# Expert weights in long rows, items of 32 slots in both layers, and 32-by-32 turns on VectorE

## The chip, the cores and the metric

The kernel runs on one core of a Trainium2 chip. The metric is the device time of one execution in microseconds (us); three timed runs of the kernel before have the median 2958.98 us. The core has TensorE (PE, with its weight loads as PEld), VectorE (DVE), ScalarE (ACT), GpSimd (POOL) and SyncE (SP), whose main work here is to issue transfers, and 16 DMA engines that carry all transfers.

## The reference, cut to what matters

The program is one block of a recurrent and sparse-attention model on 512 tokens of 1024 channels, and then two layers of a second block. Each of these two layers ends in a mixture of 32 experts, and the change lies there alone. In the first of the two layers 768 tokens (512 of the sequence, 256 of the context) go to two experts each, in the second 512 tokens:

```
for each token: the best of 4 groups, in it the 2 best of 8 experts, with two gates
run(xb, e) = (silu(xb @ w1[e]) * (xb @ w3[e])) @ w2[e]
y[token] += gate * run(token, e)
w1, w3: [2, 32, 1024, 512]    w2: [2, 32, 512, 1024]    all float32
```

One expert's weights are 6.29 MB. With the inputs of the reference, counting the routing gives 1536 chosen (token, expert) pairs over all 32 experts in the first layer, between 2 and 154 to an expert, and 1024 pairs over 26 experts in the second, where three experts have 212, 382 and 209.

## The kernel before

`route` (L1563) orders the experts by how many blocks of slots they need, and writes for every item (one block of slots, of one expert) the rows to gather, the rows to scatter to, its expert (`eid`) and whether its weights have to be loaded (`new`). A block has 64 slots in the first layer and 32 in the second (`BLOCK`). The numbers of items in the straight-line code are 41 and 51 (`NSTATIC`), which is just what the routing needs; the loop behind them runs zero times.

`experts` (L1788) works through the items. Even items take experts with many blocks from the front of the list and share one place for weights. Odd items take experts from the end and have two places by turns. A load for odd item i + 4 or even item i + 2 (`ld`) can be issued once item i has used the same piece of that place. Pieces 0 and 1 are halves of w1 and w3, pieces 2 and 3 halves of w2. Every load of a piece is issued by SP in order; where `new` is 0 the transfer is skipped. With the routing above, the first layer has 29 loads in its items, the second 23; three experts more are loaded ahead of each layer's items.

For item i the order on TensorE is: first product (pieces 0, 1; `first`, L1827), then the second product of item i - 1 (pieces 2, 3; `second`, L1843). A gather on POOL brings the item's token rows to `xg`, in ng = 128 / slots parts, so that all 128 partitions are filled. The stationary operands are slices of 64 or 32 columns, and ng such products stand side by side in the columns of the array. Both products need the tokens or the activations with channels on the partition. `turn` (L1816) does this: 128-by-128 transposes on TensorE into PSUM (`tps`), and a copy to SBUF on ACT (`xT`, `aT`). `silu` (L1835) takes one ACT and two DVE operations. `scatter` (L1853) multiplies the result by gate and modulation into `ys` on DVE (L1859), and POOL scatters it (L1860). In the first layer a DVE operation (L1858) writes the modulation into the same `ys` buffer beforehand; there are ng + 1 such buffers.

The order of instructions on each engine is that of a scheduler, except where `pin` keeps the program's order.

Of the kernel before, what the change touches and what calls it, by code (L numbers as in the profile page):

```python
# [11 lines left out]
F32 = mybir.dt.float32  # L12
# [12 lines left out]
BLOCK = (64, 32)  # L25
NSTATIC = (41, 51)
NIMAX = 64
# [5 lines left out]
def constants():  # L33
# [20 lines left out]
    # for the routing: 0.., order of experts, 8.., 256 (token tile - 128), offsets of the parts of rows, 2 p, p;  # L54
    # the work block of an item: a + total * b - places of the second lane * c
# [14 lines left out]
class Stream:  # L70
    """Column chunks of weights [1024, 256 each], split into (hi, lo) by halves of their rows, a half
    ahead of the products; the last ones are only loaded. The chunks asked for count from a base."""
# [33 lines left out]
class Kern:  # L106
# [16 lines left out]
    def rsqrt(self, pool, v, scale, eps):  # L123
        """1/sqrt(v*scale+eps) for a [128, 1] tile: a bit guess and three Newton steps, each on a
        multiple c of the root (c becomes -2 c^3), divided out in the end."""
# [21 lines left out]
    def mm3(self, out, stat, mov, start, stop):  # L147
        """out += stat.T @ mov with each side a (hi, lo) pair."""
        nc = self.nc
        (sh, sl), (mh, ml) = stat, mov  # L150
        nc.tensor.matmul(out, sh, mh, start=start, stop=False)  # L151
        nc.tensor.matmul(out, sh, ml, start=False, stop=False)  # L152
        nc.tensor.matmul(out, sl, mh, start=False, stop=stop)  # L153
# [13 lines left out]
    def wchunk(self, ap, kt, cols, pool=None, raw=None):  # L167
        """A [kt*128, cols] piece of a weight as a list of kt (hi, lo) pairs [128, cols]."""
# [68 lines left out]
    def vectors(self, z, engine):  # L237
        """Per-channel vectors with the channel on the partition."""
# [15 lines left out]
    def norm_hT(self, pool, x, gain, hi, lo, work):  # L254
        """rmsnorm of x [128, 4, 1024] (token, channel), transposed to (hi, lo) [128, 8, 512]."""
# [39 lines left out]
    def proj(self, w, N=512):  # L295
        """The two 128-channel tiles of a 256-column chunk as [channel, token] in PSUM."""
# [10 lines left out]
    def projg(self, W, c, N):  # L307
        """The same from a stream, in steps."""
# [12 lines left out]
    def fill(self):  # L321
        """One step of work that is not tied to the place where it runs."""
        if self.bg is not None:
            next(self.bg, None)
# [11 lines left out]
    def mixer(self):  # L336
        nc, tc, a = self.nc, self.tc, self.a
        with ExitStack() as st:
# [21 lines left out]
            # gates: 0.5 * sigmoid, [token, tile, 48]  # L360
# [45 lines left out]
    def keys(self, m):  # L406
        """Keys of groups 2m, 2m+1 with (hi, hi) and (lo, lo) stacked."""
# [16 lines left out]
    def compress(self, kp):  # L424
        """Compressed keys (hi, hi / lo, lo stacked) and values (two copies of the 32 rows)."""
# [57 lines left out]
    def gelu2(self, out, x, pool, shape, tag):  # L483
        """2 * gelu(x) (tanh form); x in SBUF."""
# [7 lines left out]
    def pair(self, t, Q, KD):  # L492
        """Heads 2t and 2t+1: half the gated sum of the three branches, [channel, token]."""
# [4 lines left out]
        # compressed branch  # L498
# [34 lines left out]
        # the two dense branches  # L533
# [43 lines left out]
    def rnn_vectors(self):  # L577
# [11 lines left out]
        # softplus(-lam) = max(-lam, 0) + log1p(exp(-|lam|)), exp as ((1+t)/(1-t))^16 with t = tanh(-|lam|/32)  # L589
# [9 lines left out]
        # log1p(e) = 2 atanh(z), z = e / (2 + e) <= 1/3  # L599
# [21 lines left out]
    def rnn(self, c, yA):  # L621
        """Channels 256c..: conv, RG-LRU and the mixing gates; the sum with yA to y (hi, lo)."""
# [22 lines left out]
        for m in range(2):  # L645
# [9 lines left out]
            # y = (1 + exp(log_a)) / 2 is about 1/(1-th), th = tanh(log_a / 2), and one Newton step makes it so  # L655
# [5 lines left out]
            # a = (1+th)/(1-th), sqrt(1-a^2) = 2 sqrt(-th)/(1-th)  # L661
# [23 lines left out]
    def row(self, pool, name, ap, n=D, engine=None):  # L685
        """A vector on all partitions."""
# [4 lines left out]
    def mix_out(self, xb):  # L691
        """x + rmsnorm(y @ w_out)."""
# [17 lines left out]
    def norm_add(self, x, o, g, pool):  # L710
        """x += rmsnorm(o) * g for one token tile."""
# [66 lines left out]
    def ple(self):  # L778
        """x + sigmoid(x @ w_gate + b) * (p @ w_proj), by [channel, token]; leaves x and its transpose."""
# [48 lines left out]
    def modulation(self, pool, pp, pt_pool):  # L828
        """silu(c) @ w_ada + b_ada for both conditionings, a step at a time: by rows in DRAM
        (modd) and by channel on the partition (modT)."""  # L830
# [58 lines left out]
    def mcol(self, l, r, n):  # L889
        """Modulation vector n of layer l and conditioning r, channel on the partition: [128, 8]."""  # L890
        return self.modT[l][:, r, 8 * n:8 * n + 8]

    def mrow(self, pool, l, r, n, tag, engine=None):
        """The same on all partitions: [128, 1024]."""
# [11 lines left out]
    def transposeN(self, src, n, j, tag="pp"):  # L906
        """Channel tile j of n token tiles, transposed into PSUM: [128, n * 128]."""
# [5 lines left out]
    def affine_split(self, hi, lo, src, sc, sh, pool):  # L913
        """(hi, lo) of src * sc + sh with per-partition scalars."""
# [81 lines left out]
    def open_route(self, l, NT, pool, kv):  # L996
        """What the routing keeps of each token tile, and the routers' biases."""
# [14 lines left out]
    def logit_parts(self, l, r, wg, c12):  # L1012
        """For the logits of (t scale + shift) gs + bs, which are scale (t @ wg) + shift c1 + c2."""
# [24 lines left out]
    def open_side(self, l, r):  # L1038
        """Tokens of the sequence (r = 0) or of the context (r = 1)."""
# [15 lines left out]
    def side_input(self, c):  # L1055
        """The modulated input, transposed, as (hi, lo); in the second layer with stops after the norms."""
# [40 lines left out]
    def stream(self, l):  # L1097
        """The chunks of w_in_2 and w_out_2 in the order of their use."""
# [3 lines left out]
    def tokpairs(self, W, c, NT):  # L1102
        """[token, 256] products, two token tiles to a PSUM bank."""
# [8 lines left out]
    def rope(self, out, src, i, nh, wk):  # L1112
        """Axial rotary embedding of token tile i: src [128, nh * 64] in PSUM."""
# [656 lines left out]
    def expert_load(self, l, s, n, e, cond=None, engine=None, pin=None):  # L1770
# [8 lines left out]
        for dst, src in prs:  # L1779
            src = src.rearrange("o (k p) c -> p (o k) c", p=128)  # L1780
            if cond is None:
                d = (engine or nc.sync).dma_start(dst, src)
                if pin:
                    pin(d)
# [216 lines left out]
```

## Time and profile before

| | before |
|---|---|
| median of 3 timed runs (lowest to highest) | 2958.98 us (2957.39 to 2959.16) |
| span of the profiled execution | 2959.7 us |
| PE busy, share of the span | 2529.7 us, 85% |
| DVE busy | 1376.6 us, 47% |
| ACT busy | 864.8 us, 29% |
| POOL busy | 446.9 us, 15% |
| bytes moved by DMA | 595.76 MB |
| of these, on SP's queue | 553.08 MB |

The span is the time from the first to the last instruction of one profiled execution; it is 0.7 us above the median of the timed runs. The shares are means over many stages. The two stretches with experts lie at about 1600 to 2106 us and 2470 to 2911 us of the span, and only rows from inside them tell what bounds them. "DMA share" is the mean busy share of the 16 DMA engines. It can pass 1 where packets of two queues overlap. A wait is put down to the event that came last.

### The profile page before, as it was taken

The page shows a single profiled execution, that of the slowest core. Times are in us where ns is not written, and L with a number is a line of the kernel's source. Part 1 is how long each engine was busy: PE and PEld are TensorE (multiplying, and loading weights), DVE is VectorE, ACT ScalarE, POOL GpSimd, SP SyncE. Part 2 cuts the span into 40 slices and gives each one's busy share as a digit, 9 for nine tenths or more (in the row PEclk, how much of TensorE's full clock was granted, in tenths as well). Part 3 has the DMA queues.
Part 4 walks back from the last instruction along what each step waited for, and adds up shares of the span by engine and source line. Part 5 has one row for each costly group of instructions (what it writes and reads, how often), then busy time and mean ns, then how long its engine had stood idle before and what let it go on. Part 6 is the DMA issues. An engine that isn't in the chain of part 4 may idle for free. (4 is left out here: it accounts for less than half of the span.)

```text
span 2959.7 us, 45451 instructions
## 1 busy us (share of the span) xinstructions
PE 2529.7 (85%) x17077; PEld 1696.9 (57%) x17077; DVE 1376.6 (47%) x3629; ACT 864.8 (29%) x1765; POOL 446.9 (15%) x370
## 2 busy tenths in 40 slices
PE   7899999989999979878996999998468986667773
PEld 5767767777776867777783333332157773334441
DVE  4387787653332254777765212111468763111114
ACT  2265665532221123544421111100145421011111
POOL 0010010000100000030022321111130025322212
PEclk9899999999998989889997999999779997988997
DMA  3311212337776222341157999999611167999994
GB/s 119 101 43 61 63 34 72 108 115 227 233 238 213 93 86 77 101 153 44 43 215 279 377 392 410 410 407 408 253 45 58 36 255 277 362 393 370 355 355 172
DMA packets 348716, 595.76 MB, mean 201 GB/s; under 512 B 26948, under 2 KB 180104, under 8 KB 347216
## 3 DMA queue, kind: packets, MB, share of 16 engines
q1 hardware_dynamic: 319040, 553.08, 51.7%
q0 software_dynamic: 14400, 25.59, 2.4%
q10 hardware_dynamic: 15056, 14.17, 1.6%
q8 instruction: 137, 2.24, 0.3%
q14 instruction: 83, 0.68, 0.1%
HBM read 832.37 MB, written 25.92 MB: 290 GB/s over the span
## 5 line engine op out<-in xcount | busy, mean ns | idle before, releaser
L1832 PE MATMUL ph<-r,xT 128*32 128x256 f32 (+1 forms) x4576 | 513.0, 459 | 53.8 <-DMA r<-w 50.9
L157 DVE TENSOR_TENSOR wl<-wr,wh 128x1024 fp32r<-128x1024 f32 (+1 forms) x193 | 236.6, 1230 | 315.5 <-ACT wh L156 313.1
L1832 PEld LDWEIGHTS ph<-r,xT 128*32 128x32 f32 (+1 forms) x4576 | 201.8, 122 | 305.4 <-issue 233.4
L156 ACT ACTIVATE wh<-wr 128x1024 fp32r<-128x1024 f32 (+1 forms) x193 | 202.8, 1055 | 430.4 <-PE pj L152 213.9
L1847 PE MATMUL py<-r,aT 128*32 128x256 f32 (+1 forms) x2288 | 266.5, 475 | 67.7 <-DMA r<-w 67.7
L1847 PEld LDWEIGHTS py<-r,aT 128*32 128x32 f32 (+1 forms) x2288 | 99.6, 124 | 189.4 <-issue 145.3
L1821 ACT ACTIVATE aT<-tps 128x128 f32<-128x128 f32 (+1 forms) x92 | 29.8, 324 | 585.2 <-PE tps L1819 585.2
L1839 DVE SCALAR_TENSOR_TENSOR et<-et,ph 128x128 f32<-128x128 f32 (+1 forms) x92 | 31.8, 346 | 288.8 <-ACT et L1838 288.6
L1813 POOL DMA_INDIRECT xg<-hxd,tok x92 | 96.2, 1046 | 412.0 <-PE tps L1819 380.5
L151 PE MATMUL pj<-hh,wh 128*128 128x512 f32 x384 | 155.6, 406 | 1.7 <-ACT wh L156 1.7
L152 PE MATMUL pj<-hl,wh 128*128 128x512 f32 x384 | 154.0, 401 | 0.0
L153 PE MATMUL pj<-hh,wl 128*128 128x512 f32 x384 | 153.1, 400 | 0.0
L151 PE MATMUL tk<-wh,lh 128*128 128x256 f32 x416 | 130.4, 313 | 19.4 <-DVE k2l L1168 8.0
L1860 POOL DMA_INDIRECT yd<-ys,dst x92 | 93.2, 1013 | 344.0 <-DVE ys L1859 324.6
L1858 DVE SCALAR_TENSOR_TENSOR ys<-g2s,isc,g2s 128x512 f32<-128x512 f32 x41 | 30.6, 751 | 244.3 <-DMA yd<-ys,dst 244.3
L151 PE MATMUL pj<-h2h,wh 128*128 128x512 f32 x352 | 143.5, 408 | 0.1
L153 PE MATMUL pj<-h2h,wl 128*128 128x512 f32 x352 | 139.4, 396 | 0.0
L152 PE MATMUL pj<-h2l,wh 128*128 128x512 f32 x352 | 139.2, 396 | 0.0
L153 PE MATMUL tk<-wh,ll 128*128 128x256 f32 x416 | 127.0, 305 | 2.1 <-DVE ll L157 2.1
L152 PE MATMUL tk<-wl,lh 128*128 128x256 f32 x416 | 127.3, 306 | 0.0
L540 POOL TENSOR_SCALAR B<-dm 128x512 f32<-128x512 f32 x32 | 52.7, 1647 | 451.3 <-DVE z L555 258.2
L1405 POOL TENSOR_SCALAR s2r<-s2r 128x1024 f32<-128x1024 f32 x3 | 8.3, 2775 | 666.9 <-DMA s2r<-modd 666.9
(525 smaller groups left out, 5494.8 us busy)
## 6 DMA issues: line engine op xcount, KB each, us to landing
r<-w SPq DMA_DIRECT2D x580, 1024.0 KB
wr<-w_in SPq DMA_DIRECT2D x48, 1024.0 KB
adw<-w_ada SPq DMA_DIRECT2D x96, 512.0 KB
wr<-ffn_w_gate_up SPq DMA_DIRECT2D x22, 1024.0 KB
wr<-w_out SPq DMA_DIRECT2D x16, 1024.0 KB
wr<-ffn_w_down SPq DMA_DIRECT2D x10, 1024.0 KB
fy<-yd SPq DMA_DIRECT2D x10, 1024.0 KB
wr<-ple_w_gate SPq DMA_DIRECT2D x4, 1024.0 KB
```

The lines of the kernel that those rows point to most:

```text
L151: nc.tensor.matmul(out, sh, mh, start=start, stop=False)
L152: nc.tensor.matmul(out, sh, ml, start=False, stop=False)
L153: nc.tensor.matmul(out, sl, mh, start=False, stop=stop)
L156: self.nc.scalar.activation(hi, src, AF.Copy)
L157: self.nc.vector.tensor_tensor(lo, src, hi.bitcast(F32), op=OP.subtract)
L540: nc.gpsimd.tensor_scalar(B, dm, SLOPE[h], None, op0=OP.mult)
L1813: pin(nc.gpsimd.indirect_dma_start(xg[i % XG], None, hx, bass.IndirectOffsetOnAxis(tokc.bitcast(U32), 0), bounds_check=NT * 128 * ng - 1, ...
L1832: pin(nc.tensor.matmul(H[group(g)], X[:, k % nx, group(k // nx)], R13[s][n][:, q, :, cs], start=k == 0, stop=k == 7, skip_group_check=True))
L1839: nc.vector.scalar_tensor_tensor(t, t, 1.0, H[:, 0:m], op0=OP.add, op1=OP.mult)
L1847: pin(nc.tensor.matmul(Y[group(g)], A[:, k % na, group(k // na)], R2[s][n][:, q, g * CX:(g + 1) * CX], start=k == 0, stop=k == 3, skip_gro ...
L1858: nc.vector.scalar_tensor_tensor(g, g2[1], isc, g2[0], op0=OP.mult, op1=OP.add)
L1860: d = nc.gpsimd.indirect_dma_start(yd, bass.IndirectOffsetOnAxis(dstc.bitcast(U32), 0), ys, None, bounds_check=NT * 256 * ng - 1, oob_is_e ...
```

## The change

Four things are changed together. The weights of the experts are laid out anew on the host (`expert_layout`): w1 and w3 of one half become one array of 128 rows of 4096 numbers (16 KB, where a row in memory was 2 KB before), and half of w2 becomes 128 rows of 2048 numbers (8 KB, 4 KB before), so that a piece is one transfer in place of two for pieces 0 and 1. The rows are ordered for 32-by-32 squares. The first layer gets blocks of 32 slots, as the second has, and 65 items in place of 41; by the routing this makes 30 loads in the items in place of 29. `turn` becomes one DVE instruction that turns each 32-by-32 square in place of transposes on TensorE and a copy on ACT. And the activations are turned right behind `silu`, where before their transposes stood in TensorE's queue behind the first half of the next item's first product.

```
-BLOCK = (64, 32)
-NSTATIC = (41, 51)
-NIMAX = 64
+BLOCK = (32, 32)
+NSTATIC = (65, 51)
+NIMAX = 80
...
         if n < 2:
-            r = slice(n * 512, (n + 1) * 512)
-            prs = [(self.R13[s][n][:, :, z, :], pick(w, r)) for z, w in enumerate(("w1_2", "w3_2"))]
+            dst, src = self.R13[s][n].rearrange("p q z c -> p (q z c)"), a["w13_2"][l][e, n]
         else:
-            prs = [(self.R2[s][n - 2], pick("w2_2", slice((n - 2) * 256, (n - 1) * 256)))]
-        for dst, src in prs:
-            src = src.rearrange("o (k p) c -> p (o k) c", p=128)
+            dst, src = self.R2[s][n - 2].rearrange("p q c -> p (q c)"), a["w2_2"][l][e, n - 2]
+        src = src.rearrange("o p f -> p (o f)")
...
-            def turn(src, n, tag):
-                ps = px.tile([128, 4, 128], F32, name=self.nm("tps"), tag="px")[:, 0:n]
-                for q in range(n):
-                    pin(nc.tensor.transpose(ps[:, q, :], src[:, q * 128:(q + 1) * 128], self.ident))
-                t = ek.tile([128, n, 128], F32, name=self.nm(tag), tag=tag)
-                nc.scalar.activation(t, ps, AF.Copy)
+            def turn(src, tag):
+                w = src.shape[-1]
+                t = ek.tile([128, w // BS, BS], F32, name=self.nm(tag), tag=tag)
+                nc.vector.transpose(t.rearrange("p k s -> p (k s)"), src)
                 return t
...
-                if n == 0 and i > 0:
-                    A[i - 1] = turn(H[i - 1], na, "aT")
                 if n == 1:
-                    H[i] = silu(H[i])
                     if i + 1 < NS:
-                        X[i + 1] = turn(xg[(i + 1) % XG], nx, "xT")
-                    else:
-                        A[i] = turn(H[i], na, "aT")
+                        X[i + 1] = turn(xg[(i + 1) % XG], "xT")
+                    A[i] = turn(silu(H.pop(i)), "aT")
...
+def expert_layout(w1, w3, w2):
+    w13 = np.stack([w1, w3], 3).reshape(2, 32, 4, 2, 4, 32, 2, 512).transpose(0, 1, 3, 2, 5, 4, 6, 7)
+    w2 = np.asarray(w2).reshape(2, 32, 4, 2, 2, 32, 1024).transpose(0, 1, 3, 2, 5, 4, 6)
+    return np.ascontiguousarray(w13).reshape(2, 32, 2, 128, 4096), np.ascontiguousarray(w2).reshape(2, 32, 2, 128, 2048)
```

The order of DVE's instructions in the middle of the first layer's items, before (`ph` is the first product, `et` the activation, `py` the second product; what an instruction waits for stands in brackets, DMASW being a scatter or gather):

```order
L1859 SCALAR_TENSOR_TENSOR ys_15040<-py_15029,gatem,ys_15040 128x512 [waits PE_49]
L1858 SCALAR_TENSOR_TENSOR ys_15265<-g2s_12830,isc,g2s_12829 128x512 [waits DMASW5_49,DVE_49]
L1839 SCALAR_TENSOR_TENSOR et_15093<-et_15093,ph_15049 128x256 [waits Activation_49]
L1840 SCALAR_TENSOR_TENSOR et_15093<-et_15093,ph_15049 128x256 [waits DVE_49]
L1859 SCALAR_TENSOR_TENSOR ys_15115<-py_15104,gatem,ys_15115 128x512 [waits PE_49]
```

And DVE's order at the same place of the changed kernel:

```order
L1856 SCALAR_TENSOR_TENSOR ys_15162<-py_15143,gatem,ys_15162 128x256 [waits PE_49]
L1855 SCALAR_TENSOR_TENSOR ys_15607<-g2s_12830,isc,g2s_12829 128x256 [waits DMASW0_49,DVE_49]
L1818 STREAM_TRANSPOSE xT_15313<-xg_13618 128x256 [waits DMASW1_49,PE_49]
L1836 SCALAR_TENSOR_TENSOR et_15226<-et_15226,ph_15171 128x128 [waits Activation_49]
L1837 SCALAR_TENSOR_TENSOR et_15226<-et_15226,ph_15171 128x128 [waits DVE_49]
L1818 STREAM_TRANSPOSE aT_15230<-et_15226 128x128 [waits DVE_49]
L1856 SCALAR_TENSOR_TENSOR ys_15251<-py_15232,gatem,ys_15251 128x256 [waits PE_49]
```

In both, the operation that prepares a `ys` buffer (L1858, now L1855) stands right behind the one that writes a result (L1859, now L1856). It takes over the buffer of that very result (every third of them before, every fifth now), and so waits for that result's scatter. New is that both turns stand behind it in DVE's queue; `xT` is that of the next item but one after `et`'s.

SP's issues for two neighbouring items of the second layer, before (DMAHW0 to 7 are the eight semaphores that count landings; `r` with 4x512 is half the rows of w1 or of w3, with 2x1024 half of w2; register instructions between the issues are left out):

```order
L1786 DMA r_19534<-w_2 128x4x512 [waits DMAHW5_49,PE_49]
L1786 DMA r_19534<-w_2 128x4x512 [waits DMAHW6_49]
L1786 DMA r_19535<-w_2 128x4x512 [waits DMAHW7_49,PE_49]
L1786 DMA r_19535<-w_2 128x4x512 [waits DMAHW0_49]
L1786 DMA r_20324<-w_2 128x2x1024 [waits DMAHW1_49,PE_49]
L1786 DMA r_20325<-w_2 128x2x1024 [waits DMAHW2_49,PE_49]
...
L1786 DMA r_3259_19848<-w_2 128x4x512 [waits DMAHW3_49,PE_49]
L1786 DMA r_3259_19848<-w_2 128x4x512 [waits DMAHW4_49]
L1786 DMA r_3260_19849<-w_2 128x4x512 [waits DMAHW5_49,PE_49]
L1786 DMA r_3260_19849<-w_2 128x4x512 [waits DMAHW6_49]
L1786 DMA r_19584<-w_2 128x2x1024 [waits DMAHW7_49,PE_49]
L1786 DMA r_19585<-w_2 128x2x1024 [waits DMAHW0_49,PE_49]
```

And for two neighbouring items of that layer in the changed kernel:

```order
L1783 DMA r_22260<-w_2 128x4096 [waits DMAHW3_49,PE_49]
L1783 DMA r_22261<-w_2 128x4096 [waits DMAHW4_49,PE_49]
L1783 DMA r_23045<-w_2 128x2048 [waits DMAHW5_49,PE_49]
L1783 DMA r_23046<-w_2 128x2048 [waits DMAHW6_49,PE_49]
...
L1783 DMA r_3319_22572<-w_2 128x4096 [waits DMAHW7_49,PE_49]
L1783 DMA r_3320_22573<-w_2 128x4096 [waits DMAHW0_49,PE_49]
L1783 DMA r_22310<-w_2 128x2048 [waits DMAHW1_49,PE_49]
L1783 DMA r_22311<-w_2 128x2048 [waits DMAHW2_49,PE_49]
```

An issue takes the semaphore that was used eight issues before, and waits until that transfer has landed. Two items were twelve issues and are eight now, of twice the bytes for pieces 0 and 1.

## Rows read from the trace of the kernel before

**Rows 1.** The page: span of the profiled execution.

```profile
span 2959.7 us, 45451 instructions
```

**Rows 2.** Windows, one of each layer's items: busy us, PEclk (granted clock), DMA share, GB/s.

```profile
1700.00:1800.00 100.00, 100.00 (x470) 33.63 (x468) 19.05 (x33) 11.29 (x25) 22.44 (x20) 1.00 1.02 396
2600.00:2700.00 100.00, 76.56 (x1148) 40.10 (x1144) 12.21 (x35) 11.25 (x36) 23.49 (x23) 0.90 1.02 385
```

**Rows 3.** Source lines L1832, L1847, by layer: ns min/median/max, first and last start.

```profile
L1832 PE MATMUL ph<-r,xT x1312: 592/592/1116, 1599.6 to 2096.3; 128*64 128x512 f32 x188
L1847 PE MATMUL py<-r,aT x656: 592/592/1115, 1618.1 to 2105.3; 128*64 128x512 f32 x164
...
L1832 PE MATMUL ph<-r,xT x3264: 376/379/637, 2469.6 to 2907.0; 128*32 128x256 f32 x192
```

**Rows 4.** Timeline of PE, an item of the first layer: start us, us.

```profile
1752.29 0.44 PE L1819 MATMUL tps<-ident,et 128*128 128x128 f32 x2
...
1756.24 0.66 PE L1819 MATMUL tps<-ident,xg 128*128 128x128 f32 x4
1756.83 3.65 PE L1847 MATMUL py<-r,aT 128*64 128x512 f32 x16
...
1763.85 0.44 PE L1819 MATMUL tps<-ident,et 128*128 128x128 f32 x2
```

**Rows 5.** Timeline of PE, an item of the second layer.

```profile
2650.81 0.33 PE L1819 MATMUL tps<-ident,et 128*128 128x128 f32 x1
...
2652.93 0.44 PE L1819 MATMUL tps<-ident,xg 128*128 128x128 f32 x2
2653.30 1.93 PE L1847 MATMUL py<-r,aT 128*32 128x256 f32 x32
...
2656.89 0.33 PE L1819 MATMUL tps<-ident,et 128*128 128x128 f32 x1
```

**Rows 6.** DMA, 1750 to 1950 us; q1 is SP's queue (packets, MB, share).

```profile
DMA packets 34903, 81.89 MB, mean 409 GB/s; under 512 B 2489, under 2 KB 2489, under 8 KB 34891
...
q1 hardware_dynamic: 32177, 76.11, 96.7%
```

**Rows 7.** DMA, 2600 to 2850 us.

```profile
DMA packets 39924, 94.11 MB, mean 376 GB/s; under 512 B 2805, under 2 KB 2829, under 8 KB 39894
```

**Rows 8.** DMA, 2910 to 2960 us in 40 slices; fy's rows are 8 KB.

```profile
GB/s 0 0 33 13 0 56 10 118 393 426 433 426 439 419 426 275 0 0 0 0 0 0 0 0 0 0 197 223 0 0 0 0 338 82 403 16 0 259 161 7
...
fy<-yd SPq DMA_DIRECT2D x4, 1024.0 KB
```

**Rows 9.** Waits of SP's queue, 2600 to 2860 us: us, times, longest.

```profile
SPq L1786 <- DMA r<-w: 94.0, 46, 4.0
```

**Rows 10.** Waits, 1590 to 2110 us.

```profile
DVE ys L1858 <- DMA yd<-ys,dst: 244.3, 38, 7.5
...
PE py L1847 <- DMA r<-w: 12.9, 7, 3.5
```

**Rows 11.** Waits, 2490 to 2920 us.

```profile
PE py L1847 <- DMA r<-w: 54.8, 19, 10.5
```

**Rows 12.** Timeline, one scatter of the first layer.

```profile
1806.76 0.75 DVE L1859 SCALAR_TENSOR_TENSOR ys<-py,gatem,ys 128x512 f32<-128x512 f32 x1 [2.66 <-PE py L1847]
1807.79 1.01 POOL L1860 DMA_INDIRECT yd<-ys,dst  x1 [3.38 <-DVE ys L1859]
...
1813.38 0.75 DVE L1858 SCALAR_TENSOR_TENSOR ys<-g2s,isc,g2s 128x512 f32<-128x512 f32 x1 [5.86 <-DMA yd<-ys,dst]
```

**Rows 13.** Chain of waits, the second layer's end: start us, us.

```profile
2878.83 0.06 DMA r<-w
...
2911.53 2.29 DMA yd<-ys,dst
```

**Rows 14.** DVE by form, second layer: busy, mean ns.

```profile
L1859 DVE SCALAR_TENSOR_TENSOR ys<-py,gatem,g2s 128x256 f32<-128x256 f32 x36 | 17.4, 484 | 112.6 <-PE py L1847 104.9 <-DMA yd<-ys,dst 7.7
L1839 DVE SCALAR_TENSOR_TENSOR et<-et,ph 128x128 f32<-128x128 f32 x36 | 10.4, 288 | 188.8 <-ACT et L1838 188.8
```

More of the change, by code (lines that the diff above doesn't have):

```diff
@@ L1772, in expert_load @@
         nc, a = self.nc, self.a
-        pick = lambda w, r: a[w][l][e, r, :]
         if n < 2:
-            r = slice(n * 512, (n + 1) * 512)
-            prs = [(self.R13[s][n][:, :, z, :], pick(w, r)) for z, w in enumerate(("w1_2", "w3_2"))]
-        else:
-            prs = [(self.R2[s][n - 2], pick("w2_2", slice((n - 2) * 256, (n - 1) * 256)))]
-        for dst, src in prs:
-            src = src.rearrange("o (k p) c -> p (o k) c", p=128)
[L1781 to L1784, printed above, removed]
-            else:
-                nc.sync.dma_start(dst, src, cond=cond, bounds_check="skip_entire_dma")
+            dst, src = self.R13[s][n].rearrange("p q z c -> p (q z c)"), a["w13_2"][l][e, n]
+        else:
+            dst, src = self.R2[s][n - 2].rearrange("p q c -> p (q c)"), a["w2_2"][l][e, n - 2]
+        src = src.rearrange("o p f -> p (o f)")
+        if cond is None:
+            d = (engine or nc.sync).dma_start(dst, src)
+            if pin:
+                pin(d)
+        else:
+            nc.sync.dma_start(dst, src, cond=cond, bounds_check="skip_entire_dma")
     def experts(self, l, NT, ep):
@@ L1797, in experts @@
         ng = 128 // BS
-        nx, na = 8 // ng, 4 // ng
-        CX = 128 * nx
+        na = 4 // ng
+        CX = D // ng
         XG = len(self.xg)
@@ L1803, in experts @@
             ek = st.enter_context(tc.tile_pool(name="ek", bufs=2))
-            px = st.enter_context(tc.tile_pool(name="px", bufs=2, space=PSUM))
             ph = st.enter_context(tc.tile_pool(name="ph", bufs=2, space=PSUM))
@@ L1831, in first @@
                         cs = slice(g * 128 * na, (g + 1) * 128 * na)
-                        pin(nc.tensor.matmul(H[group(g)], X[:, k % nx, group(k // nx)], R13[s][n][:, q, :, cs],
+                        pin(nc.tensor.matmul(H[group(g)], X[:, k, :], R13[s][n][:, q, :, cs],
                                              start=k == 0, stop=k == 7, skip_group_check=True))
@@ L1846, in second @@
                     for g in range(ng):
-                        pin(nc.tensor.matmul(Y[group(g)], A[:, k % na, group(k // na)], R2[s][n][:, q, g * CX:(g + 1) * CX],
+                        pin(nc.tensor.matmul(Y[group(g)], A[:, k, :], R2[s][n][:, q, g * CX:(g + 1) * CX],
                                              start=k == 0, stop=k == 3, skip_group_check=True))
@@ L1897, in experts @@
                 ld(i, n)
-            X = {0: turn(xg[0], nx, "xT")}
+            X = {0: turn(xg[0], "xT")}
             H, Y, A = {}, {}, {}
@@ L1914, in experts @@
                     pin(nc.gpsimd.tensor_tensor(t, t, self.rows[i % 2], op=(OP.mult, OP.add)[i % 2]))
-                if n == 0 and i > 0:
-                    A[i - 1] = turn(H[i - 1], na, "aT")
                 if n == 1:
-                    H[i] = silu(H[i])
                     if i + 1 < NS:
-                        X[i + 1] = turn(xg[(i + 1) % XG], nx, "xT")
-                    else:
-                        A[i] = turn(H[i], na, "aT")
+                        X[i + 1] = turn(xg[(i + 1) % XG], "xT")
+                    A[i] = turn(silu(H.pop(i)), "aT")
                 if n == 3:
@@ L1944, in experts @@
                     self.expert_load(l, 0, n, ds(e, 1))
-                xx = turn(xg[0], nx, "xT")
+                xx = turn(xg[0], "xT")
                 hh = bank(ph, "ph")
@@ L1948, in experts @@
                     first(hh, xx, 0, n)
-                aa = turn(silu(hh), na, "aT")
+                aa = turn(silu(hh), "aT")
                 yy = bank(py, "py")
@@ L1982 @@
     arrays = {n: np.ascontiguousarray(v) for n, v in inputs.items()}
+    arrays["w13_2"], arrays["w2_2"] = expert_layout(arrays.pop("w1_2"), arrays.pop("w3_2"), arrays["w2_2"])
     for n, v in constants().items():
```

## The prediction

> **What bounds the kernel now.** I read the page for the span [rows 1], then windows inside the two stretches with experts, because shares over the whole span say nothing of them. In the first layer TensorE has no idle time at all (100 us busy of 100, granted clock 1.00) and the DMA engines are full too (share 1.02) [rows 2]. In the second TensorE is busy 76.56 us of 100 and the share is the same [rows 2]. So the first layer is balanced between TensorE and transfers, and the second is bound by transfers. The waits agree: a second product waits for weights 7 times, 12.9 us in all, in the first layer [rows 10], and 19 times, 54.8 us, in the second [rows 11].
>
> Three other things are to be seen. An item of the first layer takes TensorE 1763.85 - 1752.29 = 11.56 us [rows 4], one of the second 2656.89 - 2650.81 = 6.08 us [rows 5]; a transpose group is a small part of each. The full DMA engines do not move the same in both layers: 409 GB/s in the first [rows 6], 376 in the second [rows 7], though the rows in memory have the same lengths. And DVE waits for a scatter 38 times in the first layer, 244.3 us [rows 10], which costs nothing there, since an item leaves 11.56 us for it.
>
> **The second layer.** It keeps its 51 items, 23 loads and slots; rows, issues and turns change. Its bytes are 23 x 6.29 = 144.7 MB of weights, and 2 x 1024 rows of 4 KB gathered and scattered, 8.4 MB: 153.1 MB, which at 376 GB/s are 407 us of the 437 between its first and last product [rows 3]. What rate will the long rows have? No row shows 16 KB rows of weights. The lower bound is 376, no gain. The nearest row is the loading of `fy`, whose 8 KB rows ran at 393 to 439 GB/s, mostly near 426, with nothing beside them [rows 8]. I also see why 376 could rise towards 409 with old rows: SP's queue waited 94.0 us of 260 for an earlier landing [rows 9], which is the wait for the semaphore of eight issues before. An odd item's issues here stand twelve places behind the last odd item's, with skipped ones between; so they wait for that item's last two transfers, and the engines run nearly dry once per load. With eight places they wait for the item's first transfer only, and some 4 MB are still under way. I take 418, halfway between 409 and 426: 366 us, a gain of 41; the bounds are 0 and 407 - 153.1/0.439 = 58.
>
> The transposes leave TensorE. After the last wait for weights of the regular run at 2878.83 [rows 13], five items follow at TensorE's pace. Each gets shorter by about 0.6 us (0.33 and 0.44 us of transposes that overlap a little with products [rows 5]): 3 us. Earlier they lie in waits for weights and give nothing. Together: -44 us.
>
> **The first layer's transfers.** 30 loads, 188.7 MB, and 2 x 1536 rows of 4 KB, 12.6 MB: 201.3 MB, in place of 195.0. At 418 GB/s that is 482 us; before, 195.0 MB at 409 were 477, and the stretch from the first to the last product took 1599.6 to 2105.9, 506 us [rows 3]. TensorE no longer binds: 65 items of 6.08 - 0.6 = 5.5 us are 358 us, where 41 of 11.56 were 474. So the layer changes from balanced to bound by transfers, and what matters is whether the queue stays full. It will not always. More than half of the items carry no load (an expert's second to fifth block), a place is refilled only when its item is done, so at most two odd loads and one even load can be ahead. I stepped through the 65 items with the routing of the reference: the queue runs dry at the start (the first load waits for item 1), near item 21, and near items 55 and 60, where odd items repeat an expert while the even one stays. At some 8 us an item that is 4 to 9 us each time, with restarts 35 us in all; 5 us more pass from the last landing to the last product. 482 + 40 = 522, 16 us more than before. With no dry queue it would be 487.
>
> **DVE's new queue.** In the order rows of the change, L1855 stands behind L1856 and waits for the scatter of the same buffer; behind it stand both turns and `silu`. Before, ACT did the copies, and only `silu` stood there. Per item DVE now needs: L1856 0.484 us [rows 14]; 0.28 us to POOL's start; the scatter, 1813.38 - 1807.79 = 5.59 us beside full engines [rows 12] or 2.29 us beside idle ones [rows 13]; L1855, at most the same 0.484; the two turns; and twice 0.288 us of `silu` [rows 14]. The turns have no row; I take the DVE operations of equal shape, 0.484 us for 128x256 and 0.288 for 128x128 [rows 14], with bounds of nothing and double. The Trainium skill, in "VectorE: DVE Perf Modes" (The three transpose paths), gives 311 ns for VectorE turning 128x128 in bf16; twice and once that would be 0.16 us more per item, and no run here shows it. My sum is 8.2 us per item beside full engines, 4.9 beside idle ones. Transfers need 482 / 65 = 7.4 us. So the chain lies close to the bound and steadies itself: when it is slower than the transfers, the queue drains and scatters land sooner. I take nothing for it beyond the 35 us of dry queue; at 8.2 us throughout, the layer would take 533. In the second layer no L1855 exists, and the wait is for a scatter five items back.
>
> **The rest.** `route` in the first layer works on 79 columns in place of 55: six arrays of 330 elements become 474, at about 1 ns per element (0.75 us for 512 [rows 12] and 0.484 for 256 [rows 14]) 0.9 us, say 1. Gathers and scatters grow from 41 to 65 on POOL, 1.01 us each [rows 12], 48 us more on an engine that the page has at 15%; it is the DVE wait above that shows them. The turns off TensorE and ACT cost nothing there. TensorE's granted clock should fall in the first layer from 1.00 to about the 0.90 of the second [rows 2], since it waits in both; 1.9 us of products would then take some 2.1, hidden while transfers bind.
>
> Sum: -44 + 16 + 1 = -27, from the span of 2959.7 [rows 1] to 2933, and the median lies 0.7 lower: **2932 us**.
>
> **Rivals.**
>
> *Long rows don't read faster.* For it: the rate with 2 KB and 4 KB rows is 409 already [rows 6], against 426 for 8 KB [rows 8], so only 4% is sure, in a stretch without other traffic. The second layer then gains only the 10 us of fuller issue and 3 of the tail, and the first takes 201.3/0.409 + 40 = 532, 26 more: 2959 - 13 + 26 + 1 = 2973. The Trainium skill, "DMA: Bandwidth & Descriptors" (Where 436 GB/s comes from), says that HBM's side binds such loads at about 358 GB/s per core, so that row length could not matter. By that rule neither layer would read faster; the trace does not agree, with 409 held over 200 us [rows 6].
>
> *The scatter's wait on DVE becomes the bound; this one ends slower.* A 16 KB row holds a DMA engine some eight times as long as a 2 KB row, and a scatter's small packets take turns with such rows. If each of the few turns adds 0.5 us, and the gather that now stands just ahead of the scatter in POOL's queue adds as many, 5.59 becomes 7.6 and the item 10.2 us in the full parts. It decides from a scatter of about 6.5 us on. Stepping through the items I get 20 to 50 us over my 522, thus 2950 to 2985, about 2970. Against it: two transfers that follow each other overlap, and a drained queue shortens the scatter.
>
> *The first layer gains too.* If the rows reach 432 GB/s and the queue seldom runs dry, 201.3/0.432 + 20 = 486 (-20) and the second layer 153.1/0.432 = 354 (-53 - 3): 2959 - 20 - 56 + 1 = 2884. Against it: the places for weights stay as few as they were.
>
> **How the numbers follow.** A difference of 0.2%, 6 us, is about what a measurement of this kernel can tell. My forecast (2905 to 2953) has 50%; rows without gain 14%; the scatter 20%; the first layer's gain 10%; anything else 6%. Faster: nearly all of the first, the fourth, and a quarter of the second and third: 66%. Within 0.2%: 9%. Slower: 25%. The range leaves about 1 in 10 out at each side, **2890 to 2990**; the likeliest case's own range is 2905 to 2953.
>
> **What the profile will show.** Right: `r` in whole pieces at about 420 GB/s in both layers; TensorE with waits for weights in the first layer, at a granted clock near 0.9; an item's products back to back at 5.5 us where no load is due; the second layer some 40 us shorter, the first 10 to 20 longer. DVE's L1855 waits for `yd` 60 times at 2 to 6 us. Wrong: a first layer far above 530 us, with `ph` and `py` waiting for turns in place of weights, or a second layer that still reads at 380 GB/s.

## The result, and the profile after

The changed kernel takes 2974.72 us (median of 4 runs, 2972.21 to 2977.86) against 2959.07 (2957.39 to 2960.42): ratio 1.0058, 95% interval 1.0044 to 1.0072. It is slower by 0.6%, where I forecast 0.9% faster. The loss is in the first layer's experts; the second layer gained what was forecast.

The page gives the span of the profiled execution, which answers to [rows 1]:

```profile
span 2971.6 us, 53303 instructions
```

Windows of the changed kernel: two of the first layer, one of the second, and the first layer as a whole (columns as in [rows 2]):

```profile
1700.00:1800.00 100.00, 68.55 (x1039) 40.59 (x1035) 22.21 (x66) 3.06 (x11) 22.44 (x22) 0.85 0.93 384
1800.00:1900.00 100.00, 71.40 (x1112) 45.64 (x1108) 21.78 (x66) 3.06 (x11) 22.44 (x22) 0.88 0.90 364
2600.00:2700.00 100.00, 64.72 (x1029) 37.30 (x1024) 18.14 (x54) 2.78 (x10) 22.50 (x22) 0.81 1.01 420
...
1588.00:2167.00 579.00, 406.25 (x6241) 250.17 (x6240) 129.26 (x391) 18.06 (x65) 146.43 (x134) 0.87 0.88 354
```

In the second layer the DMA engines are full and move 420 GB/s. In the first neither TensorE (406 us busy of 579) nor the DMA engines (share 0.88) are full throughout any more: something else must hold the layer up in places. The two product lines give both stretches, to be set beside [rows 3]:

```profile
L1829 PE MATMUL ph<-r,xT x4160: 376/379/637, 1588.5 to 2161.2; 128*32 128x256 f32 x199
L1844 PE MATMUL py<-r,aT x2080: 376/379/637, 1598.1 to 2166.0; 128*32 128x256 f32 x190
...
L1829 PE MATMUL ph<-r,xT x3264: 376/379/636, 2528.1 to 2920.6; 128*32 128x256 f32 x192
L1844 PE MATMUL py<-r,aT x1632: 379/379/636, 2538.6 to 2924.1; 128*32 128x256 f32 x182
```

From the start of a layer's first product to that of its last second product, the first layer takes 577.5 us (505.7 before) and the second 396.0. The same line of the kernel before, for its second layer, gives 442.4 with the start in [rows 3]:

```profile
L1847 PE MATMUL py<-r,aT x1632: 376/379/637, 2480.9 to 2912.0; 128*32 128x256 f32 x182
```

So: first layer +72, second -46, between them -2, and the first layer begins 11 us earlier (1588.5 against 1599.6), in all the 12 us between the two spans. I don't put most of those 11 us down to the change, though no run isolates them: in the thirteen profiles of this study the first layer begins anywhere between 1588 and 1600, at 1596 in the change with one order of DVE kept, and 7 of the 11 are already there at 160 us, long before the experts. In this pair of profiles they make the loss look smaller by as much.

The waits of the first layer (1590 to 2190 us; us, times, longest) answer to [rows 10]:

```profile
DVE ys L1855 <- DMA yd<-ys,dst: 412.4, 60, 10.6
...
PE py L1844 <- DMA r<-w: 35.2, 7, 11.4
```

DVE waits for a scatter in L1855 60 times, 6.9 us each; TensorE's second products wait for weights 35 us. The timeline of DVE shows one round of it, as [rows 12] did before:

```profile
1806.93 0.48 DVE L1855 SCALAR_TENSOR_TENSOR ys<-g2s,isc,g2s 128x256 f32<-128x256 f32 x1 [9.11 <-DMA yd<-ys,dst]
1807.33 0.44 DVE L1818 STREAM_TRANSPOSE xT<-xg 128x256 f32<-128x256 f32 x1
1807.69 0.25 DVE L1836 SCALAR_TENSOR_TENSOR et<-et,ph 128x128 f32<-128x128 f32 x1
1807.97 0.29 DVE L1837 SCALAR_TENSOR_TENSOR et<-et,ph 128x128 f32<-128x128 f32 x1
1808.30 0.31 DVE L1818 STREAM_TRANSPOSE aT<-et 128x128 f32<-128x128 f32 x1
1808.53 0.44 DVE L1856 SCALAR_TENSOR_TENSOR ys<-py,gatem,ys 128x256 f32<-128x256 f32 x1
1815.39 0.48 DVE L1855 SCALAR_TENSOR_TENSOR ys<-g2s,isc,g2s 128x256 f32<-128x256 f32 x1 [6.42 <-DMA yd<-ys,dst]
```

POOL's timeline of the same stretch:

```profile
1808.04 1.02 POOL L1810 DMA_INDIRECT xg<-hxd,tok  x1 [8.82 <-DVE et L1836]
1809.36 1.02 POOL L1857 DMA_INDIRECT yd<-ys,dst  x1 [0.31 <-issue]
```

and TensorE's:

```profile
1808.71 1.93 PE L1844 MATMUL py<-r,aT 128*32 128x256 f32 x32 [2.91 <-issue]
1810.43 3.66 PE L1829 MATMUL ph<-r,xT 128*32 128x256 f32 x64
1817.17 3.21 PE L1844 MATMUL py<-r,aT 128*32 128x256 f32 x28 [3.08 <-issue]
```

Read it as a loop. L1856 ends at 1808.97, its scatter starts on POOL at 1809.36 behind the next gather, and L1855 stands still until 1815.39. Only then come both turns and `silu`, so TensorE, done at 1814.09, gets its next second product at 1817.17. One round here is 1815.39 - 1806.93 = 8.46 us; 577.5 us / 65 items are 8.9, a mean of longer and shorter rounds that are told apart below. (The name "issue" ahead of that product hides the cause: `aT` was turned at 1816.76, 0.4 us before.)

### The profile page after: what moved, and what is told of

Read it like the earlier page. It is cut to its first block, busy times and chain, and to the rows that moved or that the text cites. A ratio compares the mean times of both kernels' runs of the same rounds, so it can differ in the third digit from the quotient of the medians.

```text
span 2971.6 us, 53303 instructions
## 1 busy us (share of the span) xinstructions
PE 2406.3 (81%) x20950; PEld 1769.7 (60%) x20950; DVE 1446.5 (49%) x3957; ACT 793.3 (27%) x1605; POOL 493.1 (17%) x422
## 5 line engine op out<-in xcount | busy, mean ns | idle before, releaser
L1829 PE MATMUL ph<-r,xT 128*32 128x256 f32 x7424 | 481.4, 407 | 91.8 <-DMA r<-w 87.9
L1829 PEld LDWEIGHTS ph<-r,xT 128*32 128x32 f32 x7424 | 283.2, 117 | 271.7 <-issue 95.6
L1844 PE MATMUL py<-r,aT 128*32 128x256 f32 x3712 | 274.9, 439 | 168.2 <-issue 112.2
L1844 PEld LDWEIGHTS py<-r,aT 128*32 128x32 f32 x3712 | 145.4, 125 | 277.5 <-issue 217.8
L1835 ACT ACTIVATE et<-ph 128x128 f32<-128x128 f32 x116 | 32.2, 278 | 940.1 <-PE ph L1829 551.5
L1855 DVE SCALAR_TENSOR_TENSOR ys<-g2s,isc,g2s 128x256 f32<-128x256 f32 x65 | 31.2, 484 | 412.4 <-DMA yd<-ys,dst 412.4
L1810 POOL DMA_INDIRECT xg<-hxd,tok x116 | 119.0, 1026 | 534.1 <-DVE et L1836 511.4
L1818 DVE STREAM_TRANSPOSE xT<-xg 128x256 f32<-128x256 f32 x116 | 51.1, 442 | 249.2 <-PE ph L1829 231.5
L1857 POOL DMA_INDIRECT yd<-ys,dst x116 | 117.6, 1014 | 197.8 <-DVE ys L1856 172.9
```

The lines of the kernel that those rows point to most:

```text
L1810: pin(nc.gpsimd.indirect_dma_start(xg[i % XG], None, hx, bass.IndirectOffsetOnAxis(tokc.bitcast(U32), 0), bounds_check=NT * 128 * ng - 1, ...
L1818: nc.vector.transpose(t.rearrange("p k s -> p (k s)"), src)
L1829: pin(nc.tensor.matmul(H[group(g)], X[:, k, :], R13[s][n][:, q, :, cs], start=k == 0, stop=k == 7, skip_group_check=True))
L1835: nc.scalar.activation(t, H[:, 0:m], AF.Tanh, scale=0.5)
L1844: pin(nc.tensor.matmul(Y[group(g)], A[:, k, :], R2[s][n][:, q, g * CX:(g + 1) * CX], start=k == 0, stop=k == 3, skip_group_check=True))
L1857: d = nc.gpsimd.indirect_dma_start(yd, bass.IndirectOffsetOnAxis(dstc.bitcast(U32), 0), ys, None, bounds_check=NT * 256 * ng - 1, oob_is_e ...
```

## The experiments

Eleven kernels ran. Stretches are as above, each from one profiled execution, so a few us between two of them are not clear of noise (the runs of one kernel lie up to 15 us apart); medians are of 4 runs or more, except for the one with fewer bytes (one run). The kernels before that ran beside them had medians of 2954.4 to 2956.7 us, and the ratios, which are not quite the quotients of the medians, are to those.

| kernel | median us | first layer us | second layer us |
|---|---|---|---|
| before | 2959.07 | 505.7 | 442.4 |
| after | 2974.72 | 577.5 | 396.0 |
| own buffer for L1855 | 2938.64 | 535.0 | 396.6 |
| order kept | 2939.72 | 535.0 | 396.4 |
| nine buffers | 2981.56 | 575.7 | 395.8 |
| before, own buffer | 2957.17 | 505.1 | 441.9 |
| long rows only | 2902.73 | 493.0 | 400.7 |
| one transfer, short rows | 2931.09 | 507.2 | 414.9 |
| squares only | 3045.88 | 595.4 | 447.7 |
| 32 slots, TensorE turns | 2973.12 | 565.6 | 405.8 |
| the same, own buffer | 2951.98 | 541.9 | 404.0 |
| own buffer, fewer bytes | 2835.52 | 438.3 | 394.5 |
| hybrid | 2895.01 | 493.9 | 393.5 |

**Is DVE's wait the pace?** In the change, L1855 writes a buffer of its own:

```
                 if l == 0:
-                    g = ys
+                    g = ek.tile([128, CX], F32, name=self.nm("gm"), tag="gm")
                     nc.vector.scalar_tensor_tensor(g, g2[1], isc, g2[0], op0=OP.mult, op1=OP.add)
```

> The modulation product of the first layer (L1855) gets two buffers of its own; nothing else changes. Theory A (the chain on VectorE: L1856, POOL, the scatter, L1855 behind it in the same buffer, both turns, the next products) says that this wait sets the first layer's pace: the 412 us of waits for the scatter in L1855 go to nearly nothing, and the first layer falls from 578 us to 505 to 530 us, so about 2920 us in all (2900 to 2930). Theory B (the first layer is bound by its transfers, by the queue that runs dry, or by TensorE at its lower clock, and VectorE's wait lies beside that) says that the wait goes and the layer stays above 565 us, in all within 10 us of 2975.

It takes 2938.64 us, ratio 0.9949 (0.9932 to 0.9965) to the kernel before; the first layer falls by 42.5 us to 535.0. DVE's timeline now has L1855 right behind L1856 with no wait, and what the turn waits for is TensorE's product:

```profile
1901.26 0.48 DVE L1856 SCALAR_TENSOR_TENSOR ys<-py,gatem,gm 128x256 f32<-128x256 f32 x1 [0.44 <-PE py L1844]
1901.78 0.48 DVE L1855 SCALAR_TENSOR_TENSOR gm<-g2s,isc,g2s 128x256 f32<-128x256 f32 x1
1904.71 0.45 DVE L1818 STREAM_TRANSPOSE xT<-xg 128x256 f32<-128x256 f32 x1 [2.45 <-PE ph L1829]
```

Theory A holds in kind; its layer is 5 us and its time 9 us above the bounds I gave. The waits of TensorE (1590 to 2130 us) are for weights again:

```profile
PE ph L1829 <- DMA r<-w: 114.7, 17, 17.9
...
PE py L1844 <- DMA r<-w: 36.0, 13, 9.4
```

**The control in the kernel before**, with the same edit.

> The same separate buffer in the kernel before. Theory A: its 244 us of waits for a scatter lie within items of 11.56 us of TensorE, so the waits go and the time stays, 2953 to 2965 us. If the time falls by more than 6 us, the wait cost something in the kernel before too, and the 244 us were not hidden.

2957.17 us, ratio 1.0001 (0.9991 to 1.0010); the first layer 505.1. The 244 us of [rows 10] were hidden: the same kind of wait cost nothing at 11.56 us of TensorE an item and costs 42 us at 5.2 (the item of 5.18 us below).

**Buffers or order?** Two edits of the change, each by itself:

```
-                ys = ek.tile([128, CX], F32, name=self.nm("ys"), tag="ys", bufs=ng + 1)
+                ys = ek.tile([128, CX], F32, name=self.nm("ys"), tag="ys", bufs=2 * ng + 1)
```

> The change with nine buffers for ys in the place of five; L1855 still writes into the buffer of the result. Theory A (the schedule moves L1855 ahead as far as buffers are free, nine items in the place of five, so that it always stands behind the L1856 whose scatter it waits for): the wait stays near 412 us, the first layer near 578 us, in all within 6 us of 2975. Theory B (five buffers are too few): the wait goes, the first layer falls to about 535 us, in all about 2939.

```
-                    nc.vector.scalar_tensor_tensor(g, g2[1], isc, g2[0], op0=OP.mult, op1=OP.add)
-                nc.vector.scalar_tensor_tensor(ys, Y, gate, g, op0=OP.mult, op1=OP.mult)
+                    pin(nc.vector.scalar_tensor_tensor(g, g2[1], isc, g2[0], op0=OP.mult, op1=OP.add))
+                pin(nc.vector.scalar_tensor_tensor(ys, Y, gate, g, op0=OP.mult, op1=OP.mult))
```

> The change with its five buffers, but L1855 and L1856 keep the order of the program: L1855 stands right ahead of the L1856 of its own item, behind silu and both turns, and waits for the scatter of five items before. Theory A: as with the separate buffer, the first layer about 535 us, 2933 to 2945 us in all. Theory B (the separate buffer helped in another way than by the order on VectorE): it stays above 2960.

Nine buffers leave it: 2981.56 us (half a microsecond beyond the bound I gave), and the wait of the first layer (1590 to 2190 us) stays:

```profile
DVE ys L1855 <- DMA yd<-ys,dst: 390.2, 56, 11.3
```

With nine buffers the first nine L1855 run ahead, and from then on each still stands right behind an L1856 and waits for the scatter that this one starts. Keeping the order is enough: 2939.72 us, ratio 0.9943 (0.9927 to 0.9960), with five buffers and no wait for a scatter in L1855. The DVE timeline of that kernel, where the weights are there, shows an item every 5.18 us, the turn waiting for TensorE. The DMA engines have a share of 0.98 in these 5.18 us, so they are full meanwhile:

```profile
1901.14 0.45 DVE L1818 STREAM_TRANSPOSE xT<-xg 128x256 f32<-128x256 f32 x1 [2.93 <-PE ph L1829]
...
1902.36 0.44 DVE L1855 SCALAR_TENSOR_TENSOR ys<-g2s,isc,g2s 128x256 f32<-128x256 f32 x1
1902.91 0.48 DVE L1856 SCALAR_TENSOR_TENSOR ys<-py,gatem,ys 128x256 f32<-128x256 f32 x1
1906.32 0.45 DVE L1818 STREAM_TRANSPOSE xT<-xg 128x256 f32<-128x256 f32 x1 [2.93 <-PE ph L1829]
```

**The rows and the transfers.** Long rows alone in the kernel before: 64 slots, turns on TensorE, the rows ordered by 128 channels:

```
+    w13 = np.stack([w1, w3], 3).reshape(2, 32, 2, 4, 128, 2, 512).transpose(0, 1, 2, 4, 3, 5, 6)
+    w2 = np.asarray(w2).reshape(2, 32, 2, 2, 128, 1024).transpose(0, 1, 2, 4, 3, 5)
```

> The kernel before with long rows alone: one transfer per piece of weights, rows of 16 and 8 KB per partition; items of 64 slots, turns on TensorE. Theory A (the second layer's 44 us come from the transfers): the second layer shortens by 35 to 45 us, the first by 0 to 25 because TensorE alone needs 474 of its 506 us; 2895 to 2925 us in all, about 2910. Theory B (the second layer's gain comes from turns and slots, not from rows): 2945 to 2960 us, and the second layer still reads at about 380 GB/s.

Then one transfer for each piece, but 2 and 4 KB rows:

```
+            dst, src = self.R13[s][n], a["w13_2"][l][e, n].rearrange("o q z p c -> p (o q) z c")
...
+            dst, src = self.R2[s][n - 2], a["w2_2"][l][e, n - 2].rearrange("o k p c -> p (o k) c")
```

> The kernel before with one transfer for each piece, as after the change, but rows of 2 and 4 KB in memory (w1 and w3 of a piece stand beside each other as a block, not in one row). It tells the length of a row from the number of transfers. Theory A (the rows carry the gain): second layer 435 to 445 us, first 500 to 510, 2948 to 2965 us in all. Theory B (fewer issues keep the queues fuller, and the engines reach the 409 GB/s that the first layer has): second layer 405 to 415 us, 2920 to 2935 in all.

Long rows, which come with one transfer for each piece, take 2902.73 us, ratio 0.9821 (0.9805 to 0.9838), inside the bounds of their Theory A; one transfer with short rows 2931.09, ratio 0.9923 (0.9906 to 0.9939). The same 250 us of the second layer (2560 to 2810) by the DMA view, first before, then one transfer with short rows, then long rows:

```profile
DMA packets 39904, 92.96 MB, mean 372 GB/s; under 512 B 2852, under 2 KB 2880, under 8 KB 39874
```

```profile
DMA packets 42302, 100.39 MB, mean 402 GB/s; under 512 B 2446, under 2 KB 2474, under 8 KB 42273
```

```profile
DMA packets 11925, 104.40 MB, mean 418 GB/s; under 512 B 2589, under 2 KB 2613, under 8 KB 3753
```

So the second edit's Theory B holds for the larger part of the second layer: 442.4 - 414.9 = 27.5 us come from two transfers in place of three for each half of an expert's weights, 414.9 - 400.7 = 14.2 from longer rows (in this order; long rows in three transfers were not run). The windows of the same 250 us, in the same order, show that the DMA engines were as good as full in all three, so the rate rose more than their busy share did:

```profile
2560.00:2810.00 250.00, 180.51 (x2606) 95.66 (x2606) 28.01 (x79) 24.37 (x78) 54.14 (x53) 0.88 1.00 372
2560.00:2810.00 250.00, 182.51 (x2652) 92.77 (x2656) 28.57 (x81) 25.03 (x80) 54.17 (x54) 0.87 1.03 402
2560.00:2810.00 250.00, 204.40 (x3031) 104.76 (x3035) 31.77 (x90) 28.40 (x91) 59.21 (x58) 0.90 1.00 418
```

The Trainium skill, "Perfetto Trace Analysis" (DMA Optimizations), says that batching small transfers into larger ones, of 4 or 8 KB in place of 2 KB in its example, can improve throughput dramatically. The transfers here were of 1 MB and more before: one in place of two gave 372 to 402 GB/s, 8%, and rows of 16 and 8 KB in place of 2 and 4 gave 402 to 418, 4%. In the first layer one transfer gives nothing (507.2) and long rows 12.7 us: TensorE holds it, 476.5 us busy of 493:

```profile
1594.00:2087.00 493.00, 476.52 (x2209) 159.65 (x2210) 102.16 (x165) 55.30 (x122) 97.75 (x85) 1.00 0.96 399
```

**Slots and turns.** The change without long rows (three transfers and 2 and 4 KB rows, in the order of the squares):

```
+            prs = [(self.R13[s][n][:, :, z, :], a["w13_2"][l][z, e, n]) for z in range(2)]
...
+            src = src.rearrange("o k p c -> p (o k) c")
```

> The change without its long rows: 32 slots in both layers and turns in squares of 32 on VectorE, but rows of 2 and 4 KB and three transfers per two pieces as before. Theory A: the second layer gives back all but 3 to 8 us of its 44; the first stays near 578 us, since the chain on VectorE and not the rows set its pace (560 to 590): 3005 to 3025 us in all. Theory B (rows without effect): about 2975 us. Theory C (long rows lengthen the scatter, which sets the first layer's pace): the wait of L1855 falls below 5 us and the first layer below 550.

3045.88 us, ratio 1.0293 (1.0269 to 1.0317): above all three theories. The first layer takes 595.4 us, DVE's wait is a little shorter (1580 to 2200 us; L1856 is there what L1855 is in the change; 364.3 / 60 = 6.1 us a time in place of 6.9), but the engines move only 343 GB/s with a share of 0.93 (1594 to 2191), first the wait, then the window:

```profile
DVE ys L1856 <- DMA yd<-ys,dst: 364.3, 60, 9.6
```

```profile
1594.00:2191.00 597.00, 401.95 (x6244) 237.94 (x6243) 130.88 (x391) 18.06 (x65) 146.81 (x135) 0.85 0.93 343
```

By that window the engines are busy for 0.93 x 597 = 555 us and move 205 MB, 369 GB/s while busy; the own-buffer kernel moves 411 and stands idle about as long (below). So here it is the transfers, at the rate that the second layer had before (372), which fill the layer; why items of 32 slots with three transfers read more slowly than those of 64 stays open, and what the wait costs here no run shows.

Then long rows and 32 slots with turns on TensorE (the long-rows kernel with `BLOCK = (32, 32)`, `NSTATIC = (65, 51)`, `NIMAX = 80`), without and with the separate buffer:

> Long rows, and items of 32 slots in both layers, but turns on TensorE with copies on ACT. L1855 still stands behind L1856 in the buffer of the scatter just issued. Theory A (32 slots alone put the scatter on the path: silu, which the second product waits for, stands behind L1855 on VectorE): the first layer takes 560 to 590 us, 2970 to 3000 us in all. Theory B (it takes the turns on VectorE, which put the next item's first product behind the scatter as well): the first layer takes 525 to 545 us as with the separate buffer, 2930 to 2955 in all.

> Long rows, 32 slots in both layers, turns on TensorE, and the separate buffer for L1855: what the squares are worth at 32 slots when the scatter's wait is gone. Theory A (transfers and their gaps set the rest): the first layer 530 to 545 us, like the squares with the separate buffer, 2935 to 2955 us in all. Theory B (the 1.5 us of turns and copies per item on TensorE and ACT lie on the path): 65 items by 0.6 to 1.5 us more, 570 to 630 us, 2980 or more in all.

2973.12 us (ratio 1.0056, 1.0041 to 1.0072) and 2951.98 (0.9985, 0.9975 to 0.9995). Theory A holds in both: the wait needs no turns on VectorE. It costs 565.6 - 541.9 = 23.7 us with TensorE's turns and 42.5 with the squares, which stand in DVE's queue behind L1855 too. Without the wait the squares gain 541.9 - 535.0 = 6.9 us there; of the 13 us between the two medians the second layer has 7.5.

**What sets the remaining 535 us?** The own-buffer kernel with `or (l == 0 and n > 1)` among the reasons for which `ld` loads nothing:

> The change with the separate buffer for L1855, and in the first layer without the loads of w2 behind the first three experts (the second products use what lies in their places): 62.9 MB less. It asks what sets the remaining 535 us of that layer. Theory A (transfers and the gaps in their queue): 138 MB at 420 GB/s are 330 us, TensorE's 65 items of 5.5 to 6.1 us 358 to 397; the layer takes 380 to 450 us, in all 2780 to 2855. Theory B (a chain of VectorE, POOL and TensorE of 8.2 us per item is left): the layer stays above 510 us, in all above 2910.

2835.52 us, the first layer 438.3: it follows the bytes, so transfers set at least these 97 us (Theory A). At 420 GB/s the 62.9 MB are 150 us; without them the DMA share is only 0.80 (1592 to 2031), so the layer is no longer bound by its transfers throughout.

**A better version.** The first layer of the long-rows kernel, the second of the change; in `turn`:

```
+                if l:
+                    t = ek.tile([128, 128 * n // BS, BS], F32, name=self.nm(tag), tag=tag)
+                    nc.vector.transpose(t.rearrange("p k s -> p (k s)"), src)
+                    return t
```

> Long rows in both layers; the first layer with items of 64 slots and turns on TensorE as before, the second with squares on VectorE as after the change. If the stages add up: first layer 493 us as with long rows alone, second 396 us as in the change, so 4 to 5 us less than long rows alone, about 2898 us (2890 to 2905). If the squares in the second layer cost what they did beside short rows (5 us more there), 2903 to 2910.

2895.01 us (5 runs, 2894.5 to 2897.62), ratio 0.9797 (0.9783 to 0.9810): 2.0% faster than before, and 2.7% below the change's median. The stages add up: 493.9 and 393.5.

## Why the prediction was wrong

**The step that failed** is the one on DVE's new queue: "the chain lies close to the bound and steadies itself: when it is slower than the transfers, the queue drains and scatters land sooner. I take nothing for it beyond the 35 us of dry queue". The members of the chain were named rightly; its size and, above all, its cost of nothing were wrong. It costs 42.5 us of the layer (577.5 against 535.0 with the order kept or a separate buffer; 35 to 36 between the medians), and that alone turns 2939, 0.5% faster than before, into 2975.

The trace of the change shows how, when a window is laid over each round from one L1855 to the next. From the first that waits for a scatter (1610.60 us) to the last (2147.44) there are 59 rounds. 43 of them have a DMA share of 0.80 or more; they last 10.2 us on average, and the wait for the scatter at their end is 7.9 us. The other 16 have a share below 0.80; they last 6.2 us and end in a wait of 3.9. One round of each kind, with the L1855 that ends it:

```profile
1928.48:1939.23 10.75, 6.77 (x96) 3.74 (x96) 1.98 (x7) 0.28 (x1) 2.04 (x2) 0.84 1.02 430
2038.27:2044.06 5.79, 4.01 (x40) 2.26 (x44) 1.98 (x7) 0.28 (x1) 2.04 (x2) 0.56 0.10 33
...
1939.23 0.48 DVE L1855 SCALAR_TENSOR_TENSOR ys<-g2s,isc,g2s 128x256 f32<-128x256 f32 x1 [8.70 <-DMA yd<-ys,dst]
2044.06 0.48 DVE L1855 SCALAR_TENSOR_TENSOR ys<-g2s,isc,g2s 128x256 f32<-128x256 f32 x1 [3.74 <-DMA yd<-ys,dst]
```

So scatters do land sooner when the queue has drained, as the sentence says. But a drained queue is not a cure, it is the loss: by the windows of the whole layer the engines stood idle for 12% of 579 us, some 69, in the change, and for 7% of 536 us, some 38, with the separate buffer. These 31 us are most of the 42.5; in the rest of the time the same 205 MB moved at about 402 GB/s while busy, against 411. How the wait drains the queue is my reading: with the order kept, items whose weights are there pass in 5.18 us beside full engines, so the places for later weights come free while earlier transfers are still under way; at 10 us an item they come free too late.

The size was too small even by my own rows: 5.59 us is the scatter of one round [rows 12], while the 38 waits of [rows 10] are 244.3 / 38 = 6.4 us each, 6.1 from POOL's start. And 8.2 us already lay above the 7.4 that the transfers need for an item; that called for a term in the sum. The sign of being wrong that I gave is what came: a first layer far above 530 us, with the products behind the turns.

**The scatter rival**, to which I gave 20%, is what happened. It gave 2950 to 2985, about 2970, and 10.2 us for an item in the full parts, with a scatter of 7.6 us; the 43 rounds last 10.2 us, and their wait, less the 0.39 us to POOL's start in the round shown, is 7.5. Its reason, that long rows lengthen the scatter, is borne out: in the kernel before the wait was 6.4 us, with long rows alone 302.3 / 38 = 8.0 (1590 to 2095 us), and at 32 slots it was 6.1 with short rows and 6.9 with long ones. How much of that is turns taken with long rows and how much the gather ahead of the scatter no run separates.

```profile
DVE ys L1855 <- DMA yd<-ys,dst: 302.3, 38, 9.9
```

**The first layer without the chain**: I said 522, it was 535. The gaps were right (a DMA share of 0.93 over 536 us leaves 38, I took 40); the bytes were 205 MB in place of 201, and the rate while busy 205 / 498 = 411 GB/s in place of 418:

```profile
1589.00:2125.00 536.00, 381.12 (x6240) 206.74 (x6240) 153.38 (x392) 18.04 (x65) 152.04 (x134) 0.83 0.93 382
```

That TensorE no longer binds there was right. What I didn't ask is whether 65 short items were worth it: with long rows and the 64 slots kept, the layer takes 493.0, so 32 slots with squares cost 42 us even without the wait. By the two windows, the engines are busy some 25 us longer (205 MB in place of 197) and idle some 18 us longer.

**The second layer**: -41 from the transfers and -3 from the turns were forecast, -41.7 (442.4 to 400.7) and -4.7 came. 418 GB/s was right. That the total fits is partly luck. Both sources were named, but their shares were the other way round: I ascribed 10 us to fuller issue and 31 to the rows; it was 27.5 and 14.2. And the engines did not run nearly dry once per load, as I wrote: their share was 1.02 in my own [rows 2] and 1.00 in the window above. The runs show what fewer transfers give, not that the semaphore of eight issues before is the reason. SP's wait for earlier landings is no shorter in the change (2600 to 2860 us; 94.0 us in [rows 9]):

```profile
SPq L1783 <- DMA r<-w: 117.8, 41, 5.3
```

**The turns** cost what I took, 0.75 us per item against 0.77. By form, in the first layer:

```profile
L1818 DVE STREAM_TRANSPOSE xT<-xg 128x256 f32<-128x256 f32 x63 | 27.6, 438 | 8.8 <-remote 6.3 <-PE ph L1829 2.5
L1818 DVE STREAM_TRANSPOSE aT<-et 128x128 f32<-128x128 f32 x65 | 20.2, 311 | 2.2
```

The Trainium skill, "VectorE: DVE Perf Modes" (The three transpose paths), has 311 ns for 128x128 in bf16; fp32 took the same here, and twice the columns took 1.4 times as long, not twice.

**The other parts**: six DVE operations of `route` took 0.63 to 0.64 us on 474 elements where they took 0.48 to 0.49 on 330, 0.9 us together as forecast; they lie ahead of the first layer's first product. TensorE's granted clock fell to 0.87 in the first layer, near the 0.90 that I forecast, and cost nothing that a run here separates. What stays open: beside short rows the squares made the second layer 5 us longer (447.7 against 442.4), and beside long rows 5 shorter; both are near the noise of a stretch.

## What to carry to other kernels

When an item gets shorter, go through every wait that was hidden in the old item, add up the loop of each in-order engine with its waits in it, and hold it against the new length; a loop that comes out longer than the bound belongs in the sum, not among the things that settle by themselves. If it settles because the queue of transfers runs empty, the empty queue is what it costs. An early instruction that writes into a buffer still being sent should have a buffer of its own or keep its place: more buffers only let it run further ahead into the same wait. And measure the parts of a bundled change one by one: here the layout alone was worth 1.8%, and the new slots, with the wait that they exposed, took it back.

## What the runs showed that I had not expected

Fewer transfers for the same bytes and rows raised 372 to 402 GB/s in the second layer, twice what the longer rows added, though the DMA engines had a busy share of 1.00 before. The wait for one scatter was 7.9 us in rounds beside full engines and 3.9 in the others. And nine buffers in place of five left 390 of 412 us of waits where they were.
